# All mixers ahead of all feed-forward work, with gate and up as seven block products

## The chip, the cores and the metric

The kernel runs on one core of one Trainium2 chip. The metric is the device time of one execution in microseconds. Five engines work in parallel, each through its own instructions in a fixed order: PE (matrix products), DVE (VectorE), ACT (ScalarE), POOL (GpSimd), and SP, which here only starts DMA transfers. An engine that waits for another engine's result holds up everything behind it in its own order.

## The reference

One layer over 2048 prompt tokens and 32 sample tokens (8 sequences of 4), in float32:

```python
xn = _rmsnorm(h, norm_mix)
proj = xn @ w_in                                   # q, fg, iv, og (512 columns each), ca, cg
# group A: gated linear recurrence, 4 heads, state 128 x 128, chunks of 32 tokens
o, s_new = _hgrn2_scan(silu(q), 1 - forget, iv, log(forget), s0)
o_a = _rmsnorm(o, hgrn_out_norm) * silu(og)
# group B: u = ca * sigmoid(cg), depthwise convolution of width 31, LayerNorm over channels, silu
o_b = silu(layernorm(conv(u)))
h = h + concatenate([o_a, o_b]) @ w_out
xn2 = _rmsnorm(h, norm_ffn)
h = h + (silu(xn2 @ w_ffn_gate) * (xn2 @ w_ffn_up)) @ w_ffn_down      # 1024 -> 2816 -> 1024
gate = sigmoid(_rmsnorm(h, norm_ple) @ w_ple_gate)
h = h + gate * (p @ w_ple_proj)
y = _rmsnorm(h, norm_final)
```

Outputs are `y` and the end states of the recurrence and of the convolution, for prompt and samples.

## The kernel before

Features lie on partitions and tokens run along the columns of a tile. Every float32 operand of a product is split exactly into two parts that PE takes directly (`hi` and `lo`), and `mm3` (L511 to L513) makes each product of 128 rows by 128 columns from three matmuls, `hi*lo`, `hi*hi` and `lo*hi`. Weights come as pieces of 128 x 512: a DMA fills `raw`, ACT copies its high part to `wh` (L343), DVE subtracts for `wl` (L348). `wh`/`wl` lie in a ring of ten pairs.

The 2080 tokens are eight blocks, seven of 256 and a last one of 288 (with the samples). Two neighbouring blocks, the lanes, make a superblock. Per block there are four stages. First comes the in-projection `pm<-xa,w`. Then the mixer: the recurrence, whose small matmuls go to `px` banks, and the convolution, whose 31 taps per channel tile are DVE instructions `t<-u,cvw,t` and `h<-u,cvw,h` (L351). In blocks 0 and 1 every second tap's product is made by ACT into `ct` and only added by DVE. Then come the out-projection, which reads the same tiles `xa`, and the feed-forward: gate and up from `xb`, the activation in `xc`, the down-product, and at the end the embedding gate and projection. In the superblocks 1 and 2 both lanes share one product of 512 columns; superblock 0 takes mostly 256 columns at a time, superblock 3 takes 256 and 288. The residual `h` stays in SBUF (`hbuf`, four buffers) from the load of `x` to the store of `y`.

A list written out at build time (`seq`) gives the order of the weight pieces, and so of the big products; it places the in-products of superblock s+1 between the feed-forward products of superblock s. Each superblock loads and splits every weight again. A planner (`Sched`) runs all parts of the program as generators and puts each instruction into its engine's order by its expected start. Nothing is reordered at run time.

Of the kernel before, what the change touches and what calls it, by code (L numbers as in the profile page):

```python
# [7 lines left out]
F32 = mybir.dt.float32  # L8
# [5 lines left out]
D = 1024  # L14
# [18 lines left out]
CHUNKS = (4, 4, 4, 4, 2, 4)  # L33
AW = max(CHUNKS)
SOLO = 3
# [3 lines left out]
END = 0  # L39
SPLIT = 10  # L40
WS = 0
PSP = -1
TWO = (2, 1, 2, 2)
# [8 lines left out]
FILL = 1  # L52
ACTTAPS = 2
PCT = 500
AFTER = 12
LATE = 3
# [4 lines left out]
RANK = {"o": -2.0, "d": -1.0, "u": -0.5, "q": -0.5}  # L61
# [3 lines left out]
class Buf:  # L65
    """A tile (or a slice of one) and when its last writer and readers are expected to end."""
# [8 lines left out]
    def halves(self, n):  # L75
        """Two parts of n columns each, for two users; free() gives the whole back after both."""
# [16 lines left out]
class Sched:  # L93
    """Orders the instruction streams of concurrent generators by expected start, engine by engine.

    A generator yields op(...), acq(pool, n) or wait(event)."""
# [87 lines left out]
    def run(self):  # L184
        self.advance()
        while self.ready:
            best = {}
            for i, (th, req) in enumerate(self.ready):
                s = self.start(req)
                e = req[1]  # L190
                rank = (th[3] if th[0].__name__ == "lane" else -9.0) if e == "pe" else th[1]
# [21 lines left out]
        if self.blocked or any(p.waiting for p in self.pools):  # L213
# [22 lines left out]
def trunk(ctx: ExitStack, tc: tile.TileContext, x_in, p_in, s0_in, c0_in, w_in, w_out, w_gu, w_dn,  # L236
# [6 lines left out]

    def tl(name, shape, dt=F32):
        return sb.tile(shape, dt, name=name)

# [6 lines left out]
    idn = tl("idn", [128, 128])  # L253
    mask = tl("mask", [128, 128], I32)
    mask_s = tl("mask_s", [NS, NS], I32)
    bmask = tl("bmask", [NS, NB])
    gn_, lbt_, hgg_ = Buf(tl("gn", [128, 4, KD])), Buf(tl("lbt", [128, 2, HEADS])), Buf(tl("hgg", [128, 1]))
    cvw_, cvv_ = Buf(tl("cvw", [128, 4, CONV_W])), Buf(tl("cvv", [128, 3, 4]))
    gn, lbt, hgg, cvw, cvv = gn_.ap, lbt_.ap, hgg_.ap, cvw_.ap, cvv_.ap
    lbs = Buf(tl("lbs", [128, 4, HEADS]))  # L260
    lbx, lb, ha, hb = [lbs.ap[:, i, :] for i in range(4)]
    mhalf = tl("mhalf", [128, 4])
# [6 lines left out]
    zplace = [(2, 4 * b) if b < 2 else (resb[b], 0) for b in range(NBLK)]  # L269

    def pair(name, k):
# [118 lines left out]
    def toks(n):  # L390
        return [(t, min(128, n - t)) for t in range(0, n, 128)]

# [1 line left out]
    seq = []  # L394
    AB = (0, 1)
    J = (2,)
# [1039 lines left out]
```

## Time and profile before

| | |
|---|---|
| median of 3 runs | 2679.11 us (2678.74 to 2679.26) |
| profiled execution, span of its instructions | 2677.8 us |
| PE busy | 2644.3 us (99%), 15,904 recorded matmuls |
| DVE busy | 1885.8 us (70%) |
| ACT busy | 1184.2 us (44%) |
| DMA | 287.8 MB, mean 107 GB/s |

The median lies 1.3 us above the span of the profiled execution. Times of matmuls overlap in the records, since they are pipelined; the distance between starts tells what one costs in a row of many.

### The profile page before, as it was taken

To read this page: it belongs to the slowest core of one execution; us is meant where nothing else is said; L and a number is where in the kernel's file an instruction comes from. 1 tells how busy PE (TensorE), PEld (TensorE's weight loads), DVE (VectorE), ACT (ScalarE), POOL (GpSimd) and SP (SyncE) were. 2 spreads that over 40 slices of the span, in tenths; PEclk is the share of its full clock that TensorE was granted. 3 is DMA by queue.
4 is the path that set the end of the run, shared out by engine and by line. 5 is a ranking of instruction groups with operands and counts; after the bars stand their busy time and mean duration, and the time that the engine had idled before them with its cause. 6 is when DMAs were issued, how large, how long until landed. Compare 5 with 4: busy or idle time off the path is not lost.

```text
span 2677.8 us, 43961 instructions
## 1 busy us (share of the span) xinstructions
PE 2644.3 (99%) x15904; PEld 2310.5 (86%) x15904; DVE 1885.8 (70%) x4528; ACT 1184.2 (44%) x2717; POOL 130.2 (5%) x292
## 2 busy tenths in 40 slices
PE   7999999999999999999999999999999999999998
PEld 6999999877888878788888887788788799999997
DVE  8999876599988888457457887747667674333465
ACT  6776664435454543334344543333335433222242
POOL 0110000001000010000000000000000000000000
PEclk9999999999999999999999999999999999999999
DMA  3235555422234322222234423323232342222231
GB/s 128 80 128 176 187 186 181 124 87 74 85 127 153 98 74 96 86 92 88 91 94 133 130 85 97 109 85 96 89 99 95 120 136 87 80 87 86 89 103 58
DMA packets 169131, 287.82 MB, mean 107 GB/s; under 512 B 27088, under 2 KB 36816, under 8 KB 168912
## 3 DMA queue, kind: packets, MB, share of 16 engines
q1 hardware_dynamic: 168912, 285.01, 33.5%
q8 instruction: 124, 2.03, 0.3%
q14 instruction: 95, 0.78, 0.1%
HBM read 273.51 MB, written 11.43 MB: 106 GB/s over the span
## 4 chain that ended last, share of the span: by engine, by line
PE 95%; DVE 1%; issue 1%; DMA 1%; POOL 0%; ACT 0%; SPq 0%; POOLq 0%; DVEq 0%; ACTq 0%
PE pm L511 29%; PE pm L512 29%; PE pm L513 29%; PE pm L579 1%; PE pm L581 1%; PE pm L580 1%; PE px L1233 1%; PE px L1200 1%; PE px L1229 1%; PE px L1178 1%; DVE wl L348 0%; PE px L1265 0%; PE px L1256 0%; DMA h<-x_in 0%; PE px L1302 0%
## 5 line engine op out<-in xcount | busy, mean ns | idle before, releaser
L343 ACT ACTIVATE wh<-raw 128x512 fp32r<-128x512 f32 x968 | 605.3, 630 | 774.5 <-PE pm L512 597.9
L348 DVE TENSOR_TENSOR wl<-raw,wh 128x512 fp32r<-128x512 f32 x968 | 657.8, 688 | 353.0 <-ACT wh L343 345.2
L511 PE MATMUL pm<-xbl,wh 128*128 128x256 f32 (+2 forms) x2336 | 780.3, 334 | 1.5 <-ACT wh L343 1.2
L512 PE MATMUL pm<-xbh,wh 128*128 128x256 f32 (+2 forms) x2336 | 776.2, 332 | 0.0
L513 PE MATMUL pm<-xbh,wl 128*128 128x256 f32 (+2 forms) x2336 | 774.6, 332 | 0.4 <-DVE wl L348 0.4
L511 PEld LDWEIGHTS pm<-xbl,wh 128*128 128x128 f32 x2336 | 440.1, 188 | 54.0 <-issue 7.4
L513 PEld LDWEIGHTS pm<-xbh,wl 128*128 128x128 f32 x2336 | 438.9, 188 | 44.1 <-DVE wl L348 0.9
L512 PEld LDWEIGHTS pm<-xbh,wh 128*128 128x128 f32 x2336 | 439.5, 188 | 40.6
L511 PE MATMUL pm<-xal,wh 128*128 128x256 f32 (+2 forms) x1344 | 442.7, 329 | 2.6 <-DVE xal L348 2.6
L512 PE MATMUL pm<-xah,wh 128*128 128x256 f32 (+2 forms) x1344 | 433.4, 322 | 0.0
L513 PE MATMUL pm<-xah,wl 128*128 128x256 f32 (+2 forms) x1344 | 432.4, 322 | 0.0
L511 PE MATMUL pm<-xcl,wh 128*128 128x512 f32 (+2 forms) x1056 | 357.4, 338 | 3.0 <-DVE xcl L348 2.5
L512 PE MATMUL pm<-xch,wh 128*128 128x512 f32 (+2 forms) x1056 | 353.3, 335 | 0.0
L513 PE MATMUL pm<-xch,wl 128*128 128x512 f32 (+2 forms) x1056 | 353.3, 335 | 0.0
L511 PEld LDWEIGHTS pm<-xal,wh 128*128 128x128 f32 x1344 | 254.7, 190 | 28.5 <-DVE xal L348 3.5
L512 PEld LDWEIGHTS pm<-xah,wh 128*128 128x128 f32 x1344 | 254.4, 189 | 19.2
L348 DVE TENSOR_TENSOR h<-h,pm 128x256 f32<-128x256 f32 (+1 forms) x448 | 171.4, 422 | 141.2 <-PE pm L513 137.3
L513 PEld LDWEIGHTS pm<-xah,wl 128*128 128x128 f32 x1344 | 253.6, 189 | 19.4
L511 PEld LDWEIGHTS pm<-xcl,wh 128*128 128x128 f32 x1056 | 198.8, 188 | 25.5 <-DVE xcl L348 3.4
L513 PEld LDWEIGHTS pm<-xch,wl 128*128 128x128 f32 x1056 | 198.3, 188 | 20.5
L512 PEld LDWEIGHTS pm<-xch,wh 128*128 128x128 f32 x1056 | 198.8, 188 | 18.5
L351 DVE SCALAR_TENSOR_TENSOR t<-u,cvw,t 128x256 f32<-128x256 f32 x448 | 213.0, 476 | 0.0
(151 smaller groups left out, 2421.7 us busy)
## 6 DMA issues: line engine op xcount, KB each, us to landing
raw<-w_gu SPq DMA_DIRECT2D x416, 256.0 KB, 2.8
raw<-w_dn SPq DMA_DIRECT2D x200, 256.0 KB, 2.8
raw<-w_in SPq DMA_DIRECT2D x192, 256.0 KB, 2.8
raw<-w_out SPq DMA_DIRECT2D x80, 256.0 KB, 2.8
raw<-w_pg SPq DMA_DIRECT2D x64, 256.0 KB, 2.8
h<-x_in SPq DMA_DIRECT2D x14, 512.0 KB, 5.6
y<-h SPq DMA_DIRECT2D x28, 256.0 KB, 3.2
h<-x_in SPq DMA_DIRECT2D x20, 256.0 KB, 4.4
```

The costliest lines, as they stand in the source:

```text
L343: nc.scalar.activation(out, in_, func, scale=scale, bias=bias, **kw)
L348: return op("dve", d_tt(n), lambda: nc.vector.tensor_tensor(out=out, in0=a, in1=b, op=o), R, W)
L351: return op("dve", d_tt(n, not isinstance(s, float)), lambda: nc.vector.scalar_tensor_tensor(out=out, in0=a, scalar=s, in1=b, op0=o0, op1= ...
L511: nc.tensor.matmul(out, lhsT=wh, rhs=xl, start=first, stop=False)
L512: nc.tensor.matmul(out, lhsT=wh, rhs=xh, start=False, stop=False)
L513: nc.tensor.matmul(out, lhsT=wl, rhs=xh, start=False, stop=last)
L579: nc.tensor.matmul(bank.ap, lhsT=xs[0], rhs=wl, start=(k == 0), stop=False)
L580: nc.tensor.matmul(bank.ap, lhsT=xs[0], rhs=wh, start=False, stop=False)
L581: nc.tensor.matmul(bank.ap, lhsT=xs[1], rhs=wh, start=False, stop=(k == KD - 1))
L1178: nc.tensor.matmul(bs.ap[:, c], lhsT=kb.ap[:, c], rhs=q.ap[:, c], start=True, stop=True)
L1200: nc.tensor.matmul(bu[e].ap[:, c], lhsT=kt.ap[p, c], rhs=V[i].ap[p, hc], start=True, stop=True)
L1229: nc.tensor.matmul(bo.ap[:, c], lhsT=scst.ap[:, c], rhs=V[i].ap[:, hc], start=True, stop=False, skip_group_check=True)
```

## The change

The program now has two parts. In the first, all four superblocks go through in-projection, mixer and out-projection only. Superblock 0 loads and splits the weights as before and also writes both parts of each piece to DRAM (`wcache`); superblocks 1 to 3 read both parts from there and split nothing. The mixer's results have operand tiles of their own (`xo`), so in-products of s+1 can stand between the mixers and the out-products of s. All taps run on DVE. Each two feature tiles of the residual go to DRAM (`h1d`) after the out-products. Out-products of the last superblock are placed after the mixers' tiles have been freed (event `ffn`).

In the second part the 2080 tokens are three passes of 696, 696 and 688, each as two halves of 348 (or 344) columns. For gate and up of one 128-column tile of the hidden layer, the four blocks (gate and up, lower and upper half of the 1024 inputs, here `g0 g1 u0 u1`) times the four blocks of the operand (two halves of the inputs, two halves of the tokens) are made by seven block products instead of eight, in Winograd's form of Strassen's scheme. `combine` makes the seven operands per input tile from the normalised residual, `split2` makes the seven weight combinations, `gate_up` multiplies in the order `A12 A11 S1 S2 S4 S3 A22`, and `z_copies`, `z_low`, `z_high` make the sums. Down-product, embedding gate and projection are plain products for each half. Tiles of the second part reuse the first part's memory.

```diff
-CHUNKS = (4, 4, 4, 4, 2, 4)
+CHUNKS = (4, 4, 4, 4, 4, 2)
+HALF = (348, 348, 344)
+COMBOS = ("A12", "A11", "S1", "S2", "S4", "S3", "A22")
+NRING = 9
+NRAW = 6
-ACTTAPS = 2
...
     def split_weights():
+
         for i, (s, u, lanes) in enumerate(seq):
...
+                if not s:
+                    yield wait(("raw", i, a))
+                    raw = raw_of.pop((i, a))
+                    yield from split_piece(raw, hi, lo)
+                    S.release(raws, raw)
+                    S.spawn(keep_weights(kept, (hi, lo), ("kept", u, a)), 0)
+                else:
+                    yield wait(("kept", u, a))
+                    for c, t in zip(kept, (hi, lo)):
+                        yield dma(t.ap.bitcast(F32), c, W=[t], nbytes=512 * 512)
...
+            if s == NSUP - 1 and kind == "o":
+                yield wait("ffn")
...
+    def store_h1(b, m):
         n = blk_n(b)
...
+        idx = resb[b]
+        yield dma(h1d[:, m:m + 2, b * BLK:b * BLK + n], hbuf[idx][:, m:m + 2, 0:n], R=H[idx][m:m + 2],
+                  nbytes=1024 * n)
...
+    def gate_up(t, c, j, before):
+
+        z = (t, c, j)
+        bc = yield acq(main)
+        yield from strassen(*z, 0, "A12", bc, True)
+        if before:
+            yield from before
+        ba = yield acq(main)
+        yield from strassen(*z, 1, "A11", ba, True)
+        bb = yield acq(main)
+        S.spawn(z_copies(z, ba, bb), -3)
+        S.spawn(z_low(z, bc, bb), 0)
+        S.spawn(z_high(z, ba), 0)
+        yield from strassen(*z, 2, "S1", bb, True)
+        yield wait(("zc", z, "p1"))
+        yield from strassen(*z, 3, "S2", ba, False)
+        yield wait(("zc", z, "p5"))
+        yield from strassen(*z, 4, "S4", bb, False)
+        yield wait(("zc", z, "u2"))
+        yield from strassen(*z, 5, "S3", ba, False)
+
+        def rest():
+            yield wait(("zc", z, "c22"))
+            yield from strassen(*z, 6, "A22", ba, False)
+
+        return rest()
...
+    def z_copies(z, ba, bb):
+        n = HALF[z[0]]
+        for i, name, bank in ((1, "p1", ba), (2, "p5", bb), (3, "u2", ba)):
+            yield wait(("zp", *z, i))
+            q = yield acq(tmp2)
+            yield act(q.ap[:, 0:n], bank.ap[:, 0:n], AF.Copy, R=[bank], W=[q], n=n)
+            zt[z, name] = q
+            S.fire(("zc", z, name))
...
+    def z_high(z, ba):
+        n = HALF[z[0]]
+        yield wait(("zp", *z, 5))
+        yield wait(("zc", z, "p5"))
+        p5 = zt.pop((z, "p5"))
+        p5a = p5.ap[:, 0:n]
+        yield tt(p5a, ba.ap[:, 0:n], p5a, ALU.add, R=[ba, p5], W=[p5], n=n)
+        S.fire(("zc", z, "c22"))
...
+        yield from put(a12, "A12")
+        yield from put(a11, "A11")
+        yield sum_(s, a21, a22, ALU.add)
+        yield from put(s, "S1")
+        yield from put(a22, "A22")
+        S.release(tmp2, a22)
+        yield sum_(a21, a11, a21, ALU.subtract)
+        yield sum_(a11, s, a11, ALU.subtract)
+        yield from put(a11, "S2")
+        yield sum_(s, a12, a11, ALU.subtract)
+        S.release(tmp2, a12, a11)
+        yield from put(s, "S4")
+        S.release(tmp2, s)
+        yield from put(a21, "S3")
+        S.release(tmp2, a21)
...
+    S.fire("ffn")
+    S.spawn(load2(), 1)
+    S.spawn(split2(), SPLIT)
```

How instructions move shows at three places. The first is PE's order around the LayerNorm of the last block. `px<-idn,h` with 128x128 or 32x128 are transposes of the convolution's result `h` to tokens and, in the second group, back; `xb` is gate and up's operand. Before:

```order
L1041 MATMUL px_173<-idn,h_74 128x128 x4
L1041 MATMUL px_176<-idn,h_74 128x128 x4
L1041 MATMUL px_174<-idn,h_74 32x128 x4
L511 MATMUL pm_172<-xbl,wh_94 128x512
L512 MATMUL pm_172<-xbh,wh_94 128x512
L513 MATMUL pm_172<-xbh,wl_95 128x512
...
L1073 MATMUL px_175<-idn,h_74 128x128 x2
L1073 MATMUL px_175<-idn,u_124 128x32
```

After, with `xa` the last in-products' operand and `xo` that of the out-products:

```order
L527 MATMUL pm_174<-xah,wl_95 128x288
L1136 MATMUL px_177<-t_151,t_149 32x128 x2
L1145 MATMUL px_176<-t_148,t_153 128x256
...
L921 MATMUL px_176<-idn,h_78 128x128 x4
L921 MATMUL px_177<-idn,h_78 128x128 x4
L921 MATMUL px_175<-idn,h_78 32x128 x4
L1182 MATMUL px_176<-idn,t_146 128x128 x2
...
L953 MATMUL px_175<-idn,u_144 128x32
L525 MATMUL pm_171<-xol,wh_96 128x256
```

Before, 51 big matmuls of 512 columns stand between the two groups of transposes. After, nothing but small matmuls of the mixers (55 rows) stands between the last in-product and the first out-product.

The second place is DVE at the step into the feed-forward of a superblock. Before, the rows are from superblock 0: `h` is scaled by the norm (L351) and `xbl`, the low part of gate and up's operand, follows:

```order
L348 TENSOR_TENSOR wl_89<-raw_103,wh_88 128x512
L351 SCALAR_TENSOR_TENSOR h_75<-h_75,gn,px_173 128x256 x2
L351 SCALAR_TENSOR_TENSOR t_128<-h_72,gn,px_175 128x256
L351 SCALAR_TENSOR_TENSOR t_129<-h_72,gn,px_175 128x256
L351 SCALAR_TENSOR_TENSOR t_133<-h_72,gn,px_175 128x256
L351 SCALAR_TENSOR_TENSOR t_127<-h_72,gn,px_175 128x256
L348 TENSOR_TENSOR xbl<-t_128,xbh 128x256
```

After, from the last residual addition of the out-products (`h_78`, 288 columns) into pass 0; `f` and `h_77` hold squares of `norm2`, and the two reductions are the sums of the first half's tokens:

```order
L373 TENSOR_TENSOR h_78<-h_78,px_177 128x288
L373 TENSOR_TENSOR tw_105<-raw_102,tw_105 128x512
L373 TENSOR_TENSOR wl_89<-tw_105,wh_88 128x512
L373 TENSOR_TENSOR f_9008<-f_9008,h_77 128x348
L373 TENSOR_TENSOR wl_87<-raw_100,wh_86 128x512
L373 TENSOR_TENSOR f_9007<-f_9007,f_9008 128x348
L1613 MEMSET sm_68 128x1
L373 TENSOR_TENSOR wl_91<-raw_101,wh_90 128x512
L1622 TENSOR_REDUCE sm_68<-px_178 128x2
L1625 TENSOR_REDUCE sm_68<-px_178 92x1
L376 SCALAR_TENSOR_TENSOR h_77<-h_77,f_9009 128x348
```

The whole norm of pass 0 and all of `combine` follow the last out-products in this order, and no big product of another stage is left for PE in between.

The third place is PE in one gate and up tile of pass 0, with bank and buffer numbers; the rows shown are the first matmul of each block product, and each stands for twelve (four input tiles by three):

```order
L1354 MATMUL px0_175<-xal_107,wh4_88 128x348
...
L1354 MATMUL pm0_171<-xal_107,wh5_90 128x348
...
L1354 MATMUL px0_175<-xal_107,wh6_92 128x348
...
L1354 MATMUL pm0_171<-xal_107,wh7_94 128x348
...
L1354 MATMUL pm1_172<-xal_107,wh0_80 128x348
...
L1354 MATMUL pm0_171<-xal_107,wh8_96 128x348
```

Two banks now alternate block by block within a tile, and between two block products into the same bank its content is copied by ACT or added by DVE; before, a bank took its 24 matmuls in a row and was then evacuated. The fifth row is the next tile's first product, placed ahead of this tile's last.

## Rows read from the trace of the kernel before

**Rows 1.** The page: busy time of each engine, and PE's granted clock in 40 slices.

```profile
PE 2644.3 (99%) x15904; PEld 2310.5 (86%) x15904; DVE 1885.8 (70%) x4528; ACT 1184.2 (44%) x2717; POOL 130.2 (5%) x292
...
PEclk9999999999999999999999999999999999999999
```

**Rows 2.** The page: chain that ended last, by engine and by line.

```profile
PE 95%; DVE 1%; issue 1%; DMA 1%; POOL 0%; ACT 0%; SPq 0%; POOLq 0%; DVEq 0%; ACTq 0%
PE pm L511 29%; PE pm L512 29%; PE pm L513 29%; PE pm L579 1%; PE pm L581 1%; PE pm L580 1%; PE px L1233 1%; PE px L1200 1%; PE px L1229 1%; PE px L1178 1%; DVE wl L348 0%; PE px L1265 0%; PE px L1256 0%; DMA h<-x_in 0%; PE px L1302 0%
```

**Rows 3.** Windows: stretch, length, busy time of each engine, clock, DMA share, GB/s.

```profile
0.00:67.00 67.00, 53.34 (x326) 46.86 (x327) 58.59 (x169) 46.66 (x108) 6.64 (x22) 1.00 0.40 127
67.00:134.00 67.00, 67.00 (x568) 63.65 (x567) 63.17 (x174) 49.90 (x135) 11.24 (x28) 1.00 0.25 80
134.00:200.00 66.00, 66.00 (x562) 64.06 (x561) 60.79 (x153) 49.46 (x126) 7.52 (x18) 1.00 0.39 127
...
2200.00:2400.00 200.00, 200.00 (x1597) 199.78 (x1596) 86.10 (x173) 60.52 (x120) 1.23 (x1) 1.00 0.28 90
```

**Rows 4.** Timeline of PE at the start: start, duration, line and tiles.

```profile
14.84 0.58 PE L511 MATMUL pm<-xal,wh 128*128 128x256 f32 x1 [2.43 <-DVE xal L348]
...
17.40 0.41 PE L512 MATMUL pm<-xah,wh 128*128 128x256 f32 x1
...
18.89 0.41 PE L513 MATMUL pm<-xah,wl 128*128 128x256 f32 x1
```

**Rows 5.** Timeline of the end.

```profile
2665.06 0.29 PE L513 MATMUL pm<-xch,wl 128*128 128x288 f32 x1
...
2670.72 3.49 DVE L351 SCALAR_TENSOR_TENSOR h<-h,gn,px 128x288 f32<-128x288 f32 x8 [1.95 <-PE px L839]
2671.68 2.88 SPq L462 DMA_DIRECT2D y<-h  x4
```

**Rows 6.** Timeline of PE in two stretches of big products.

```profile
1149.66 0.39 PE L511 MATMUL pm<-xbl,wh 128*128 128x512 f32 x1
...
1155.93 0.39 PE L511 MATMUL pm<-xbl,wh 128*128 128x512 f32 x1
...
2249.96 0.30 PE L511 MATMUL pm<-xbl,wh 128*128 128x288 f32 x1
...
2251.96 0.28 PE L511 MATMUL pm<-xcl,wh 128*128 128x256 f32 x1
...
2254.79 0.30 PE L511 MATMUL pm<-xbl,wh 128*128 128x288 f32 x1
```

**Rows 7.** Groups by line and shape, PE: the feed-forward's products, one line of three.

```profile
L511 PE MATMUL pm<-xbl,wh 128*128 128x512 f32 x992 | 396.2, 399 | 0.0
...
L511 PE MATMUL pm<-xbl,wh 128*128 128x256 f32 x928 | 261.2, 281 | 1.5 <-ACT wh L343 1.2 <-DVE h L348 0.2
...
L511 PE MATMUL pm<-xcl,wh 128*128 128x512 f32 x480 | 191.7, 399 | 0.0
...
L511 PE MATMUL pm<-xbl,wh 128*128 128x288 f32 x416 | 122.9, 295 | 0.0
...
L511 PE MATMUL pm<-xcl,wh 128*128 128x256 f32 x384 | 109.0, 284 | 3.0 <-DVE xcl L348 2.5 <-DVE h L348 0.3
...
L511 PE MATMUL pm<-xcl,wh 128*128 128x288 f32 x192 | 56.7, 295 | 0.0
```

**Rows 8.** Groups by line and shape, DVE: weight low parts and taps.

```profile
L348 DVE TENSOR_TENSOR wl<-raw,wh 128x512 fp32r<-128x512 f32 x968 | 657.8, 688 | 353.0 <-ACT wh L343 345.2
L351 DVE SCALAR_TENSOR_TENSOR t<-u,cvw,t 128x256 f32<-128x256 f32 x448 | 213.0, 476 | 0.0
...
L351 DVE SCALAR_TENSOR_TENSOR h<-t,cvw,h 128x32 f32<-128x32 f32 x60 | 14.6, 244 | 0.0
```

**Rows 9.** Timeline of DVE: two taps one behind the other.

```profile
90.95 0.88 DVE L351 SCALAR_TENSOR_TENSOR t<-u,cvw,t 128x256 f32<-128x256 f32 x2
```

**Rows 10.** Costliest groups, ACT: weight high parts.

```profile
L343 ACT ACTIVATE wh<-raw 128x512 fp32r<-128x512 f32 x968 | 605.3, 630 | 774.5 <-PE pm L512 597.9
```

More of the change, by code (lines that the diff above doesn't have):

```diff
@@ L182, in start, with run @@
         return t
-    def run(self):
+    def run(self, last=True):
         self.advance()
@@ L487, in load_weights @@
             src = unit_src(u)
-            for a in range(pieces(u)):
+            for a in range(2 if not s else 0):
                 raw = yield acq(raws)
@@ L916, in stage_x @@
     def stage_x(b):
-        for x in range(b - 1):
-            yield wait(("lnread", x))
+        yield wait(("n1", 1, HOLD))
         for k in range(0, KD, 4):
@@ L1341, in trunk, with cut, flat @@
     S.spawn(lane(1), 30)
-    with tc.manual_schedule():
-        S.run()
+    manual = tc.manual_schedule()
+    manual.__enter__()
+    S.run(False)
+    assert len(tmp.free) == 8 and len(hg.free) == 10 and len(misc.free) == 4
+    scope["guard"].__exit__(None, None, None)
+    open_scope("ffn")
+    def cut(tiles, count):
+        return [tuple(Buf(t[:, i * WID:(i + 1) * WID]) for t in tiles) for i in range(count)]
+    def flat(i, count):
+        f = hbuf[i].rearrange("p k t -> p (k t)")
+        return [Buf(f[:, j * WID:(j + 1) * WID]) for j in range(count)]
@@ new lines, in mm3s, with strassen @@
+    def mm3s(out, wh, wl, xh, xl, first, last):
+        for i, (a, b) in enumerate(((wh, xl), (wh, xh), (wl, xh))):
+            nc.tensor.matmul(out, lhsT=a, rhs=b, start=first and i == 0, stop=last and i == 2, skip_group_check=True)
+    def strassen(t, c, j, i, name, bank, first):
+        n = HALF[t]
+        key = ("z", t, c, j, i)
+        yield wait(("w2", key))
+        w = w2.pop(key)
+        for kp in range(KP):
+            yield wait(("x2", t, kp, name))
+            x = X2[kp][name]
+            col = slice(kp * 128, (kp + 1) * 128)
+            args = (bank.ap[:, 0:n], w[0].ap[:, col], w[1].ap[:, col], x[0].ap[:, 0:n], x[1].ap[:, 0:n],
+                    first and kp == 0, kp == KP - 1)
+            yield op("pe", 3 * d_mm(n), lambda a=args: mm3s(*a), R=[*w, *x], W=[bank])
+        S.release(ring, w)
+        S.fire(("zp", t, c, j, i))
@@ new lines, in row, with norm2, get @@
+    def row(n, get, r, ev):
+        bank = yield from rms2(n, get)
+        yield act(r.ap[:, 0:n], bank.ap[:, 0:n], AF.Copy, R=[bank], W=[r], n=n)
+        S.release(misc, bank)
+        S.fire(ev)
+    def norm2(t):
+        if t:
+            yield wait(("a", t - 1, 2, 0, 1))
+        for h in HALVES:
+            def get(k, h=h):
+                q = yield acq(tmp2)
+                yield from h1_load(t, h, k, q)
+                return q, q
+            yield from row(HALF[t], get, r2[h], ("r2", t, h))
+        if t:
+            yield wait(("a", t - 1, last_chunk, CHUNKS[-1] - 1, 1))
+        for kp in range(KP):
+            five = yield acq(tmp2, 5)
+            S.spawn(combine(t, kp, five), 0)
```

730 lines of the change are left out of this document (481 added, 249 removed).

## The prediction, made before the changed kernel ran

> **What bounds the kernel now.** I read the busy times first: PE is busy for 2644.3 of 2677.8 us, at full clock in every slice [rows 1]. The chain that ended last says the same from the other side: 95% of it is PE, and 87% are the three lines of `mm3` [rows 2]. Then I read windows, because DVE's 70% is an average over unlike stretches: in the first 200 us, where convolution and weight splitting meet, DVE is busy for 182.6 us (58.59 + 63.17 + 60.79), 91%, and late in the feed-forward for 86 of 200 [rows 3]. So the time is the number of matmuls times their pace, plus a start of 14.8 us [rows 4] and an end of 12.6 us, from the end of the last product (2665.06 + 0.13) to 2677.8 [rows 5]. The change must show itself as fewer columns through PE, and as new stretches in which PE has nothing to do.
>
> **What it removes and adds on PE.** The pace is taken start to start. With 512 columns, 27 intervals lie between 1149.66 and 1155.93: 0.2322 us. With 288, 15 between 2249.96 and 2251.96: 0.1333. With 256, 24 between 2251.96 and 2254.79: 0.1179 [rows 6]. The three lie close to a line, which gives 0.160 us at 348 columns and 0.158 at 344, widths that no row shows. If a column cost what it costs at 512, a pass would be cheaper by 1.1%; as at 288, dearer by 1%.
>
> Feed-forward products before, each row three times for the three lines [rows 7]: (992 + 480) x 3 = 4416 of 512 columns, 1025 us; (928 + 384) x 3 = 3936 of 256, 464 us; (416 + 192) x 3 = 1824 of 288, 243 us. Sum 1732.6. After, one pass has 22 tiles x 7 block products x 4 input tiles x 3 = 1848 for gate and up (eight blocks would be 2112), 22 x 8 x 2 x 3 = 1056 for down, 8 x 8 x 2 x 3 = 384 for the embedding gate and 96 for its projection: 3384. Two passes at 0.1598 and one at 0.1580 make 1616.2 us (1598 to 1632 by the two bounds). That is **116 us less**. Of it 126 us come from the eighth block (792 matmuls x 0.16); the change of widths gives back 10.
>
> The rest of PE's stretch, 2665.2 - 14.8 - 1732.6 = 917.8 us, is the mixers' products, the small matmuls and whatever small waits there are. The mixers' products keep their number and widths, so I keep it. Start, this rest and the new feed-forward make 2548.8 us. Now the stretches without cover.
>
> **Mixers alone.** DVE loses most weight splits there: only 64 pieces are split, three quarters of the mixers' pieces come back from DRAM. It gains the taps that ACT made. In the changed order 2207 DVE instructions stand ahead of the last out-products. A tap takes 476 ns [rows 8], but two in a row end after 0.88 us [rows 9], so each costs 0.40 start to start; the same 0.07 is taken off the others. 928 taps make 371 us, 116 sample taps at 0.17 make 20, 64 low parts at 0.61 make 39. The other 1099 lie between 0.17 (narrow) and 0.42 (256 columns); I take 0.29, 319 us. Sum about 750 us, or 820 at the 91% density of [rows 3], against some 855 us at which PE ends its last in-product (14.8 + 917.8, less 48 for the last out-products, 192 of 256 and 192 of 288 columns, and some 30 for small matmuls of the feed-forward). PE stays ahead, narrowly. Only in superblock 0, which also splits, is DVE late: its work up to the last tap of block 1 comes to some 252 us, which is 288 us after the start at that density, LayerNorm included, where PE has run through what it was given at about 281; with the transposes and splits behind it I take **18 us** (0 to 45). In-products of s+1 stand right behind those of s and read the same `xa`, so at three places PE waits for the first splits: **5 us** (0 to 20).
>
> Superblock 0 reads 256 KB and writes 512 KB for each piece, 49 MB in some 280 us, 175 GB/s; the trace moved 127 GB/s at a share of 0.40 [rows 3], so the queues would be near 0.55 busy, and I put nothing on it.
>
> **The last mixer.** Before, 51 products of 512 columns cover the LayerNorm of the last block (the first order above), nearly 12 us. After, PE has only small matmuls there. DVE has 146 instructions left after the last in-product: 31 wide taps (12.4 us), 60 narrow (10), 55 others at 0.28 (15), 38 us together; transposes back, activation and split add 6. About 10 of these 44 us are small matmuls already counted in the rest: **34 us** (15 to 55).
>
> **Into the feed-forward.** After the last addition of the out-products, DVE's order (second place above) has the end of the norm of pass 0, first for one half, then the other: reductions, power on POOL, broadcast. At the end of the program that chain takes 5.5 us from the last product to the first scaled tile [rows 5]; two of them with copies between make 14. Then `combine` stands: some 39 DVE instructions ahead of the fourth `A12`, at 0.45, 18 us. **32 us** (20 to 50): the products have nothing else to do. Later passes have the previous pass's embedding and down-products as cover, so they cost nothing unless the operands' tiles come free late. A cold clock comes with both idle stretches: products of 256 columns at the start take (18.89 - 17.40)/7 = 0.213 us, nearly double [rows 4], until about 6 us after the first; half of such a stretch is lost each time, **6 us** for two.
>
> **Within the feed-forward.** Per tile DVE has seven low parts and four differences of weights (11 x 0.61) and seven operations of 348 columns (0.44): 9.8 us, against 84 x 0.16 = 13.4 on PE. ACT has seven high parts of 630 ns [rows 10] and seven operations of 348 columns, some 7 us. Neither is the bound. A copy between two block products of one bank has the twelve matmuls of the other bank as cover, 1.92 us; it takes about 0.45, behind at most one other instruction of 0.69. I take **8 us** for all 66 tiles and the pass ends (0 to 70).
>
> **The end.** 5.5 us of chain, 16 scalings of 348 columns at 0.5 (before: 8 in 3.49 us [rows 5]) and a store of 3: **17 us**.
>
> Sum: 2548.8 + 18 + 5 + 34 + 32 + 6 + 8 + 17 = 2668.8 us of span. The median lies 1.3 us above the profiled span, so **2670 us**.
>
> At 512 columns the trace has a product each 0.232 us [rows 6]. A rule of the Trainium skill would have it faster: "TensorE: Matmul & The Clock Gate", section "Back-to-back issue gap", gives a lone stream of matmuls of N columns N/2.4 ns plus 2.5 at full clock, 216 ns at 512. The trace disagrees. By that rule 348 columns would take 147.5 ns and the feed-forward's products about 1492 us, an estimate from that page.
>
> **The rivals.**
>
> *The waits are mostly hidden (20%).* The estimates of 34 and 32 us assume DVE works through its order without gaining on PE. If the out-products already cover most of the norm, and DVE is done with the taps when the last in-product ends, 15 and 15 remain, and superblock 0 costs nothing. 2548.8 + 5 + 15 + 15 + 4 + 5 + 16 = 2609; with half of that saving 2640. I name 2625.
>
> *The mixers become DVE-bound (13%).* 750 us of DVE work, less the 38 behind, must end with PE's last in-product at about 855 + 18 + 5. That holds down to a density of 0.83. At 0.78, with more waits between engines than in [rows 3] because no feed-forward fills the gaps, it ends 45 us later: 2715.
>
> *Each gate and up tile waits (13%); slower than before.* Each tile has four waits for ACT or DVE under a cover of 1.92 us, in engines that are over half full and in fixed order. If the releasing instruction stands behind two weight operations of 0.6 us, the wait is not covered. At 0.22 us each, 264 waits make 58 us, less the 8: 2720. From 0.065 us each on (17 us in all) the kernel is no faster than before.
>
> *The pace gets better (2%).* At full clock, 2.4 GHz, 512 columns at one a cycle take 0.213 us and 348 take 0.145; [rows 6] stand 0.019 above that at 512, 0.013 at 288 and 0.011 at 256. If most of this excess hangs on the order of banks and weights and goes with the new one, the products save up to 0.015 x 10,152 = 150 us: 2520. Nothing in the rows speaks for it; the excess is there in both stretches. The page's rule above is a milder form of this case.
>
> **How the numbers follow.** 52% remain for my sum, with a range of its own of 2650 to 2692. A change below 0.2%, 5.4 us, can hardly be told from none: same is 2673.8 to 2684.5. Of my own case about half lies below, three tenths within, a fifth above. Faster: 0.27 + 0.20 + 0.02 and a small part of the DVE case, 0.51. Same: 0.16 + 0.02, 0.18. Slower: 0.31. The range reaches from the hidden case's lower half to the slower rivals: **2612 to 2720**.
>
> **What would show it.** Products of 348 columns at 0.160 us start to start; 10,152 of them. PE idle of 20 us or more at three places: out-products of superblock 0, behind the last in-product (ended by `xo`), ahead of the first block product (ended by `xa`). Between block products no idle over 0.1 us in most tiles. DVE at 85% to 92% through the mixers. I am wrong if `z_copies` or the `c22` addition ends many waits of PE, if PE's idle in the mixers is spread over in-products and named DVE, or if the three places together stay under 40 us.

## The result and the profile after

The changed kernel takes 2725.1 us (median of four runs, 2720.45 to 2728.98), the kernel before on the same chip 2679.2. The ratio is 1.0171, with an interval of 1.0157 to 1.0186: **slower by 46 us**, where 2670 had been forecast. The profiled execution has a span of 2723.3 us and a mean granted clock of 0.968.

The page: engine, busy time, share of the span, instructions; then the granted clock in 40 slices, and the chain that ended last.

```profile
PE 2566.1 (94%) x15886; PEld 2409.8 (88%) x15886; DVE 1999.1 (73%) x4506; ACT 1071.4 (39%) x2397; POOL 134.1 (5%) x286
...
PEclk9999899999998679999999899999999999999998
...
PE 89%; DVE 6%; DMA 2%; POOL 1%; ACT 1%; issue 1%; SPq 0%; DVEq 0%; POOLq 0%; ACTq 0%
```

PE lost 78 us of busy time against [rows 1], and still the span grew by 45.5: PE now stands still for 157.2 us where it stood still for 33.5. The clock row shows where (a slice is 68.1 us): dips in slice 5 (272 to 340 us), in slices 13 to 15 (817 to 1021) and in slice 23 (1498 to 1566), the end of the first pass. The windows were laid around these and around the end (stretch, its length, busy time and count of PE, PEld, DVE, ACT and POOL, granted clock, DMA share, GB/s):

```profile
0.00:281.00 281.00, 263.67 (x1799) 232.74 (x1800) 255.91 (x696) 134.62 (x364) 34.12 (x92) 0.99 0.66 228
281.00:300.00 19.00, 9.64 (x63) 7.40 (x61) 18.93 (x51) 5.59 (x17) 3.18 (x6) 0.74 0.21 69
300.00:600.00 300.00, 298.56 (x1559) 242.81 (x1560) 246.91 (x682) 93.66 (x283) 38.07 (x78) 0.99 0.60 199
600.00:860.00 260.00, 256.13 (x1649) 219.60 (x1648) 199.13 (x592) 72.25 (x215) 29.18 (x69) 1.00 0.52 166
700.00:800.00 100.00, 99.34 (x595) 81.60 (x594) 64.05 (x203) 16.27 (x50) 6.15 (x21) 1.00 0.59 187
860.00:935.00 75.00, 44.61 (x182) 28.09 (x182) 56.04 (x190) 15.64 (x53) 8.12 (x23) 0.59 0.27 76
985.00:1036.00 51.00, 17.47 (x69) 14.37 (x69) 37.56 (x84) 21.60 (x48) 1.71 (x2) 0.60 0.42 130
1482.00:1512.00 30.00, 19.50 (x102) 18.22 (x101) 30.00 (x65) 20.02 (x44) 0.00 (x0) 0.77 0.21 63
2698.00:2723.30 25.30, 3.52 (x17) 2.05 (x15) 13.02 (x31) 1.33 (x3) 1.70 (x2) 0.61 0.36 112
```

Up to 860 us PE is short of work once only, around 281. Then come 75 us with PE busy for 45, and 51 us with 17. The eye should stop at 700 to 800: PE is full, but DVE, which has the convolution to do, is busy for 64 of 100 us, and 70 us later PE has run out of work. What PE's waits are called (engine, line, what it waited for: us in total, times, longest):

```profile
PE px L1136 <- DMA t<-s_in: 22.8, 8, 4.4
PE pm L1354 <- DVE xal L373: 14.9, 3, 8.6
PE px L1618 <- DVE sm L1613: 14.2, 3, 7.6
PE pm L527 <- DVE wl L373: 14.1, 2, 8.7
PE pm L525 <- ACT wh L368: 10.3, 1, 10.3
...
PE px L1354 <- DVE h L373: 5.5, 9, 0.6
...
PE pm L1354 <- DVE h L373: 1.8, 3, 0.6
...
PE pm L1354 <- DVE f L373: 1.2, 2, 0.6
```

L1136 multiplies by the recurrence's states of the samples, which are loaded for the purpose (`s_in`). L1354 is the block product, L1618 the transposes in a norm's sum over features. The last three rows are the wait for `c22`: fourteen times, 8.5 us in all, in 66 tiles. They stand only at tiles with a down-product behind them, where no product of a next tile is placed ahead of the last block product; there are fifteen of these.

The mile-posts, from PE's timeline (start, duration, engine, line, operation):

```profile
867.51 0.29 PE L527 MATMUL pm<-xah,wl 128*128 128x288 f32 x1
...
871.34 0.42 PE L1136 MATMUL px<-t,t 128*32 128x128 f32 x1 [3.54 <-DMA t<-s_in]
...
934.05 0.58 PE L525 MATMUL pm<-xol,wh 128*128 128x256 f32 x1
...
1200.03 0.33 PE L525 MATMUL px<-xol,wh 128*128 128x348 f32 x1
...
1203.70 0.32 PE L527 MATMUL pm<-xoh,wl 128*128 128x348 f32 x1
...
2698.44 0.32 PE L527 MATMUL pm<-wh,wl 128*128 128x344 f32 x1
```

The last in-product starts at 867.51 and the first out-product 66.5 us later. Between 1200.03 and 1203.70 lie 23 intervals of 0.1596 us. The last product starts at 2698.44, and 24.7 us follow from its end to the span's. The last out-product starts at 984.44; the first block product starts at 1006.9, and the hundredth at 1042.9, where a hundred in a row would need 15.8.

What happens in this gap, from the timelines of SP, ACT and DVE (`h`, `f` hold loaded residual tiles and squares; `r` is the norm):

```profile
990.14 0.91 SPq L454 DMA_DIRECT2D h<-h1d  x2
...
991.87 0.46 ACT L368 ACTIVATE r<-px 128x348 f32<-128x348 f32 x1 [3.90 <-PE px L1633]
994.39 0.98 ACT L368 ACTIVATE h<-h 128x348 f32<-128x348 f32 x2 [2.06 <-DMA h<-h1d]
995.38 1.50 ACT L368 ACTIVATE f<-f 128x348 f32<-128x348 f32 x3
...
995.91 0.52 DVE L376 SCALAR_TENSOR_TENSOR h<-h,f 128x348 f32<-128x348 f32 x1 [5.91 <-ACT f L368]
...
1003.36 2.06 DVE L376 SCALAR_TENSOR_TENSOR f<-f,gn,r 128x348 f32<-128x348 f32 x4 [2.36 <-ACT r L368]
...
1006.32 0.94 DVE L373 TENSOR_TENSOR xal<-f,xah 128x348 fp32r<-128x348 f32 x2
```

The first half's norm is done at 992.3. SP issues the second half's eight loads only from 990.1 on, and its squares, sums and reductions follow the first half's norm: each load waits for a free buffer in `get`, and the two halves follow each other in one generator.

The end of the first pass, DVE:

```profile
1482.84 1.07 DVE L376 SCALAR_TENSOR_TENSOR hxl<-h,gn,hxh 128x348 fp32r<-128x348 f32 x2
1483.82 0.51 DVE L373 TENSOR_TENSOR xal<-h,xah 128x348 fp32r<-128x348 f32 x1
1484.25 0.51 DVE L373 TENSOR_TENSOR f<-h,f 128x348 f32<-128x348 f32 x1
1484.68 0.51 DVE L373 TENSOR_TENSOR h<-pm,h 128x348 f32<-128x348 f32 x1
...
1505.56 0.68 DVE L373 TENSOR_TENSOR wl<-raw,wh 128x512 fp32r<-128x512 f32 x1
```

DVE is busy for all 30 us of this window. The next pass's operands (`xal`, `f<-h,f`) stand among the last residual additions and the operand of the embedding gate (`hxl`), all ahead of the embedding's first `wl` at 1505.56; PE gets its weights 10.3 us late. At the third pass's end, where no next pass follows, 5.4 us of such a wait remain (2619.57).

The very end, SP's queue of stores, the row that answers to the last of [rows 5]:

```profile
2705.47 15.53 SPq L454 DMA_DIRECT2D y<-h  x32
```

Where four stores were issued after the last norm, 32 now are, 0.485 us each; DVE is through with its 16 scalings (7.82 us) before half of the stores are out.

### The profile page after: what moved, and what is told of

It reads as the page before. It is cut to its first block, busy times and chain, and to the rows that moved or that the text cites. A ratio compares the mean times of both kernels' runs of the same rounds, so it can differ in the third digit from the quotient of the medians.

```text
span 2723.3 us, 43381 instructions
## 1 busy us (share of the span) xinstructions
PE 2566.1 (94%) x15886; PEld 2409.8 (88%) x15886; DVE 1999.1 (73%) x4506; ACT 1071.4 (39%) x2397; POOL 134.1 (5%) x286
## 4 chain that ended last, share of the span: by engine, by line
PE 89%; DVE 6%; DMA 2%; POOL 1%; ACT 1%; issue 1%; SPq 0%; DVEq 0%; POOLq 0%; ACTq 0%
PE pm L1354 20%; PE pm L525 14%; PE pm L527 13%; PE pm L526 13%; PE px L1354 12%; PE px L525 3%; PE px L527 3%; PE px L526 3%; DVE h L373 1%; PE pm L593 1%; PE pm L595 1%; PE pm L594 1%; DVE h L376 1%; DMA t<-s_in 1%; PE px L1113 1%; PE px L1080 1%
## 5 line engine op out<-in xcount | busy, mean ns | idle before, releaser
L373 DVE TENSOR_TENSOR wl<-raw,wh 128x512 fp32r<-128x512 f32 x520 | 356.4, 689 | 200.0 <-ACT wh L368 197.1
L368 ACT ACTIVATE wh<-raw 128x512 fp32r<-128x512 f32 x520 | 323.2, 627 | 380.7 <-PE pm L526 208.2
L527 PE MATMUL pm<-xoh,wl 128*128 128x348 f32 (+4 forms) x1072 | 350.0, 326 | 14.1 <-DVE wl L373 14.1
L525 PE MATMUL pm<-xol,wh 128*128 128x348 f32 (+4 forms) x1072 | 353.7, 330 | 1.9 <-DVE xol L373 1.6
L526 PE MATMUL pm<-xoh,wh 128*128 128x348 f32 (+4 forms) x1072 | 349.6, 326 | 0.0
L1354 PE MATMUL pm<-xal,wh 128*128 128x348 f32 (+1 forms) x661 | 213.6, 323 | 18.0 <-DVE xal L373 14.9
L527 PEld LDWEIGHTS pm<-xoh,wl 128*128 128x128 f32 x1072 | 205.5, 192 | 20.3 <-DVE wl L373 14.7
L368 ACT ACTIVATE wh<-tw 128x512 fp32r<-128x512 f32 x198 | 124.8, 630 | 244.2 <-DVE tw L373 120.5
L525 PEld LDWEIGHTS pm<-xol,wh 128*128 128x128 f32 x1072 | 205.7, 192 | 12.1 <-issue 3.8
L1354 PE MATMUL pm<-xah,wh 128*128 128x348 f32 (+1 forms) x661 | 212.6, 322 | 0.0
L1354 PE MATMUL pm<-xah,wl 128*128 128x348 f32 (+1 forms) x661 | 212.4, 321 | 0.0
L526 PEld LDWEIGHTS pm<-xah,wh 128*128 128x128 f32 x960 | 182.1, 190 | 12.1
```

Source lines behind the costliest of these rows:

```text
L368: nc.scalar.activation(out, in_, func, scale=scale, bias=bias, **kw)
L373: return op("dve", d_tt(n), lambda: nc.vector.tensor_tensor(out=out, in0=a, in1=b, op=o), R, W)
L525: nc.tensor.matmul(out, lhsT=wh, rhs=xl, start=first, stop=False)
L526: nc.tensor.matmul(out, lhsT=wh, rhs=xh, start=False, stop=False)
L527: nc.tensor.matmul(out, lhsT=wl, rhs=xh, start=False, stop=last)
L1354: nc.tensor.matmul(out, lhsT=a, rhs=b, start=first and i == 0, stop=last and i == 2, skip_group_check=True)
```

## The experiments

Theory: PE's saving is real, and it is lost in stretches where no product covers the chain of the other engines; what sets such a stretch is the order in which DVE, ACT and the loads come, not how much DVE has to do. Rival: DVE has too much to do in all (1999 us busy), and order only moves the loss. Differences between kernels are taken from the ratios, times 2679 us; the kernel before took 2678.8 to 2680.1 in the three sets. A ratio's interval reaches some 4 us to either side, so a difference of 5 us is not clear of the noise.

**The samples' states a step ahead.** The load of the next state is issued before the work on this one:

```diff
-            for g in range(4):
+            def state(g):
                 s0 = yield acq(tmp)
...
+                return s0, s3
+            ahead = yield from state(0)
+            for g in range(4):
+                s0, s3 = ahead
+                if g < 3:
+                    ahead = yield from state(g + 1)
```

> Edit: the samples' old states are loaded one step ahead, so that each load has a tile of its own and stands ahead of the store of the step before. In the changed kernel PE waits 22.8 us in 8 waits for these loads. Theory 1 (the lost time is PE's stretches without cover, and they add up): the stretch behind the last in-product shrinks from 66 us to 42 to 48 us, the kernel comes to 2698 to 2710. Rival (the stretch is bound by DVE's taps, which fill it as well): it shrinks by less than 6 us, 2717 to 2725.

Measured: 1.0154 (1.0138 to 1.0171), 2721.5 us. PE's waits from 860 to 940 of this kernel:

```profile
PE px L921 <- DVE h L373: 9.6, 2, 6.2
PE px L953 <- DVE h L384: 4.3, 2, 2.3
PE px L1143 <- DMA t<-s_in: 4.2, 3, 2.5
```

The wait for the states fell from 22.8 us to 4.2, and the kernel gained 4.6, which is not clear of the noise. The stretch from the last in-product to the first out-product (868.4 to 932.8) is 64 us long, where it was 66.5. That is what the rival expected: the convolution's result (`h`, L921 transposes it) now comes last. Its window says why:

```profile
890.00:920.00 30.00, 14.45 (x45) 7.29 (x44) 25.81 (x98) 3.72 (x13) 2.77 (x4) 0.50 0.18 46
```

DVE is busy for 25.8 of 30 us. Two chains of nearly one length end here, and the largest row of the waits named only the later one.

**Loads of pass 0 on ACT's queue, both halves side by side.**

```diff
-                yield from h1_load(t, h, k, q)
+                yield from h1_load(t, h, k, q, dma if t else dma_a)
...
-            yield from row(HALF[t], get, r2[h], ("r2", t, h))
+            if t:
+                yield from row(HALF[t], get, r2[h], ("r2", t, h))
+            else:
+                S.spawn(row(HALF[t], get, r2[h], ("r2", t, h)), 0)
```

> Edit: the loads of the first pass's norm and operands are issued by ACT instead of SP, both halves at once, so that norm and operand sums stand among the last out-products in DVE's order. Theory 1: the idle between the last out-product and the first block products (50 us until all four input tiles are there) falls to 10 to 20 us, 2685 to 2700. Rival (DVE or the loads are the limit in this stretch anyway): under 10 us saved, 2714 to 2725.

Measured: 1.0154 (1.0139 to 1.0169), 2720.7 us: 4.6 us, again within the noise, a miss. The first block product does come earlier, at 997.3 and 0.6 us behind the last out-product, but the out-products took 61.4 us (50.4 in the changed kernel), with 5.5 us of waits for their weights from DRAM. ACT's timeline shows that the edit put load and use on one engine, each use ahead of the next load:

```profile
951.99 0.49 ACT L371 ACTIVATE h<-h 128x348 f32<-128x348 f32 x1 [2.23 <-DMA h<-h1d]
952.00 0.35 ACTq L460 DMA_DIRECT2D h<-h1d  x1
954.30 0.49 ACT L371 ACTIVATE h<-h 128x348 f32<-128x348 f32 x1 [1.82 <-DMA h<-h1d]
954.31 0.38 ACTq L460 DMA_DIRECT2D h<-h1d  x1
```

**Chunks of the hidden layer in the order of before.**

```diff
-CHUNKS = (4, 4, 4, 4, 4, 2)
+CHUNKS = (4, 4, 4, 4, 2, 4)
```

> Edit: the last two down-product chunks change places (4 then 2 tiles becomes 2 then 4), so the last down-product of a pass has 192 matmuls (30.7 us) in place of 96 (15.4 us) over the same 16 residual additions and 16 operand splits on DVE (16 us). Theory 1: the three waits at the ends of the passes (10.3, 8.7 and 5.4 us) go, with the cold clock behind them 25 to 40 us, 2685 to 2700. Rival (the waits there come from the norm's chain or from weights): no more than 8 us, 2715 to 2725.

Measured: 1.0173 (1.0158 to 1.0188), 2725.4 us: nothing gained. The 5.4 us of the third pass's end are gone; around the first pass's end waits of 7.0, 4.5 and 3.0 us (`wl`, a norm's power, `h`) stand in place of the 10.3.

**Eight plain products in place of seven.** The order of the two parts stays; gate and up are made by `mm3` with the 16 operands of before:

```diff
-        yield from strassen(*z, 0, "A12", bc, True)
...
+        for up_ in range(2):
+            for h in HALVES:
+                bank = yield acq(main)
+                for i in range(2):
+                    for kp in range(KP):
...
+                        yield op("pe", 3 * d_mm(n), lambda a=args: mm3(*a), R=[*w, *x], W=[bank])
+                S.spawn((u_plain if up_ else g_plain)(z, h, bank), 0)
```

> Edit: gate and up as eight plain block products (1.14 times their matmuls: 792 more, 126 us) in the same two-part program, no combinations of weights and operands. Theory 1 (the seven products save what their count says, the loss lies elsewhere): 2823 to 2850, a little under +126 since DVE has less to do at the start and the ends of the passes. Rival (waits between block products of one bank eat the saving): +60 or less, 2725 to 2785.

Measured: 1.0520 (1.0504 to 1.0536), 2818.6 us, 93 us more than with seven. The 792 matmuls are worth 126 at 0.16; some 33 come back. At the start of the feed-forward 8 do (from the last out-product the hundredth product lies 34.9 us further than its own time, not 42.6). PE's waits at the ends of the passes are 11 us less, and the 9 us in the tiles are gone; the other 5 are not traced. So the seven products cost a quarter of what they save, and the new order of the stages, with plain products, is 139 us slower than before, of which the change of widths is 10.

**Out-products of superblock 2 later.** Eight more in-product units of the last superblock come first, so that its convolution gets its inputs earlier:

```diff
-        add(s + 1, todo[:AFTER], then)
+        after = 20 if s == NSUP - 2 else AFTER
+        add(s + 1, todo[:after], then)
```

> Edit: the out-products of superblock 2 stand behind 20 of the last superblock's 24 in-product units instead of behind 12. In the changed kernel DVE is idle for a third of 700 to 800 us, while these out-products run and no convolution has its input, and the taps of the last two channel tiles start only at 858.6 and 890.2. Theory 2 (the end of the mixers is late because DVE gets its last inputs late, not because it has too much work): the first out-product of the last superblock starts 15 to 25 us earlier, 2700 to 2710. Rival (DVE's sum of work decides): under 5 us, 2719 to 2725.

Measured: 1.0126 (1.0111 to 1.0141), 2713.0 us, 12 us less than the changed kernel and a little short of the expectation. The window of 700 to 800:

```profile
700.00:800.00 100.00, 97.28 (x642) 83.28 (x642) 75.08 (x232) 20.95 (x66) 9.64 (x28) 0.97 0.52 157
```

DVE is busy for 75 us, not 64, and the first out-product of the last superblock starts at 922.2, 12 us earlier. So 11 of DVE's 36 us of idle time there were want of inputs. After the last in-product's start DVE has 27.6 us of work left, where it had 49.1.

**Loads ahead and both halves at once at the start of the feed-forward.** A loader of its own runs ahead on SP's queue, and `combine` issues its four loads before its first scaling:

```diff
+    def ahead0():
+        for k in range(KD):
+            for h in HALVES:
+                q = yield acq(tmp2)
+                yield from h1_load(0, h, k, q)
...
+        if t == 0:
+            S.spawn(ahead0(), -5)
...
             yield from h1_load(t, h, k, q)
+        for q, k, h in ((a21, kp, 1), (a22, kp + KP, 1), (a11, kp, 0), (a12, kp + KP, 0)):
             qa = q.ap[:, 0:n]
```

> Edit: in the first pass the 16 loads of the norm go out ahead of their use, both halves side by side, and the four loads of an input tile's operands stand ahead of its first scaling; in the run with ACT's queue the squares still came one load at a time, some 2 us each. Theory 2 (the start of the feed-forward is a chain of load, square, load): the first block product starts at most 8 us after the last out-product and idle before steady products is 15 us or less in place of 50, 2690 to 2705. Rival (DVE's work for norm, operands and weights is the limit, about 45 us of it): 2712 to 2722.

Measured: 1.0109 (1.0094 to 1.0124), 2708.9 us, 16.6 us less and 4 above the expected range. The first block product starts at 985.98, directly behind the last out-product at 985.85. What waits remain there:

```profile
PE pm L1354 <- DVE xal L373: 9.5, 1, 9.5
PE pm L1354 <- DVE x2l L373: 6.4, 1, 6.4
```

The norm is hidden; `combine`, one operand after the other, is not.

**The next pass's operands after the embedding's first result.**

```diff
             yield wait(("a", t - 1, last_chunk, CHUNKS[-1] - 1, 1))
+            yield wait(("h3", t - 1, 0, 1))
```

> Edit: the operands of the next pass are made only after the first embedding output, not between the last down-product and the embedding. In the changed kernel DVE is busy without a gap from 1482 to 1512 with the sums and splits of the next pass standing among the residual additions, and the embedding's first weights wait behind them. Theory 2 (order on DVE at the pass end, not the amount): the waits of 10.3 and 8.7 us at the first two pass ends fall under 4 us each, 2700 to 2712. Rival (the same DVE work only moves to the start of the next pass and PE waits there): 2719 to 2727.

Measured: 1.0203 (1.0188 to 1.0219), 2734.1 us: 9 us more. From 1440 to 1570 PE waits 5.3 us for `wl` and 7.2 us, in three waits, for ACT's `f` (L368), the activation of an embedding gate, which frees a bank and now stands behind the splits of the next pass's operands. The sum is the 12 us of before under other names. The rival had expected this at the start of the next pass; it came within the embedding.

**The four together** (states ahead, out-products later, loads ahead, operands later):

> All of the last three edits and the prefetch of sample states together. Theory 2: the savings add, 2640 to 2670, faster than the kernel before. Rival (the stretches hide one another): 2690 or more.

Measured: 1.0057 (1.0040 to 1.0074), 2696.7 us, 30.5 us less than the changed kernel, a miss: the time lies in the rival's range. Its reason does not hold, though. Singly the four sum to 4.6 + 12.1 + 16.6 - 8.6 = 24.7, so they do not hide one another; they were worth less than expected.

**Convolution inputs first.** In the last superblock all products that feed the convolution's first channel tile (`ca0 cg0`) come first and the others between those of the recurrence; with later out-products, states and loads ahead, without the later operands:

```diff
+        if s == NSUP - 2:
+            todo = []
+            for w in "ca0 cg0 iv f0 q0 ca1 cg1 f1 q1 ca2 cg2 f2 q2 ca3 cg3 f3 q3 og0 og1 og2 og3".split():
+                todo += [(w[:2].rstrip('0123'), int(w[-1]))] if w[-1] in '0123' else [(w, j) for j in range(4)]
```

> Edits: prefetched sample states and the early loads of the first pass (as in the runs before), and in the last superblock the in-products start with the first convolution tile's two units, with the out-products of superblock 2 after 20 units; the operands of the next pass are left where the changed kernel has them. Theory 2 (the three edits that order DVE's work earlier add, the fourth gave 9 us back): 2683 to 2692. Rival (the stretches hide one another, as the late operands' pass ends did not): 2697 or more.

Measured: 0.9997 (0.9988 to 1.0006), 2679.0 us, 4 below the expected range: **order alone gives back all 46 us**, with DVE busy for 1996.3 us, hardly less than before. The last in-product starts at 881.3, the first out-product at 904.5: 23 us, where 66.5 lay, and DVE has 16.2 us of work in them. The hundredth block product starts at 992.5, 50 us earlier, so the whole gain lies ahead of it. The window of 860 to 935, at a granted clock of 0.84 where it was 0.59:

```profile
860.00:935.00 75.00, 63.95 (x425) 55.63 (x424) 43.50 (x133) 18.55 (x49) 4.06 (x10) 0.84 0.65 204
```

**The same with the chunks of before.** Only `CHUNKS = (4, 4, 4, 4, 2, 4)` is added:

> The kernel of e9 with the last two down-product chunks exchanged (2 then 4 tiles). In e3 that took away the wait at the end of the third pass (5.4 us) and moved those of the other two. With the operand loads out of the way the same DVE work stands behind 192 matmuls. Theory 2: 5 to 12 us under e9. Rival (DVE's amount at a pass end is the limit): within 3 us of e9.

Measured: **0.9946 (0.9933 to 0.9960), 2666.5 us, faster than both kernels**. Its page, the row of busy times:

```profile
PE 2550.8 (96%) x15886; PEld 2401.2 (90%) x15886; DVE 1998.7 (75%) x4506; ACT 1073.6 (40%) x2397; POOL 133.2 (5%) x286
```

Its window from 700 to 800:

```profile
700.00:800.00 100.00, 99.40 (x681) 84.49 (x680) 85.10 (x259) 25.51 (x78) 11.79 (x36) 1.00 0.53 160
```

PE's timeline at its step into the feed-forward:

```profile
961.53 0.29 PE L532 MATMUL pm<-xoh,wl 128*128 128x288 f32 x1
961.66 0.32 PE L1366 MATMUL pm<-xal,wh 128*128 128x348 f32 x1
```

DVE's busy total is that of the changed kernel (1998.7 against 1999.1), and the time is 60 us less. From 700 to 800 DVE is busy for 85 us. The edit that gave nothing by itself gives 14 here. In the trace the hundredth block product starts at 997.75, 5 us later than without it, though the edit concerns only the down-products: the planner places everything anew. The gain comes behind, where PE's waits from 1000 us on sum to 34.0 us instead of 41.5. Why the same edit did nothing in the changed kernel no run shows.

**Sums of operands on POOL.** The kernel with convolution inputs first, with `sum_` moved from DVE (16 sums a pass):

```diff
-            return tt(out.ap[:, 0:n], a.ap[:, 0:n], b.ap[:, 0:n], o, R=[a, b], W=[out], n=n)
+            return op("pool", 700.0, lambda: nc.gpsimd.tensor_tensor(
+                out=out.ap[:, 0:n], in0=a.ap[:, 0:n], in1=b.ap[:, 0:n], op=o), [a, b], [out])
```

> The kernel of e9 with the four operand sums of each input tile (16 a pass, 128x348) on POOL instead of DVE. It takes 7 us of work from DVE at each pass start, where DVE is busy without a gap. If DVE's amount is the limit there: 8 to 15 us under e9. If POOL's longer instruction or its latency stands in the chain: the same or up to 20 us over e9.

Measured: 1.0035 (1.0022 to 1.0047), 2689.6 us, 10 us more than with the sums on DVE. The sums lie in the chain, and POOL's part of it is longer (POOL's busy time rose by 55 us for 48 sums, about 1.1 us each, against 0.51 on DVE). DVE was not relieved either: it has 48 instructions fewer and is busy for 2005.5 us, where it was busy for 1996.3. Beside a sum on POOL its own instructions take longer:

```profile
982.46 1.25 POOL L1708 TENSOR_TENSOR f<-h,f 128x348 f32<-128x348 f32 x1 [0.52 <-DVE x2l L373]
982.84 1.25 DVE L373 TENSOR_TENSOR x2l<-f,x2h 128x348 fp32r<-128x348 f32 x1
...
984.61 0.51 DVE L373 TENSOR_TENSOR x2l<-f,x2h 128x348 fp32r<-128x348 f32 x1
```

So this run does not test what less work for DVE is worth.

**No low parts of the feed-forward's weights.** The changed kernel, with some 650 of DVE's instructions left out:

```diff
-                        yield from split_piece(src, *e)
+                        yield act(e[0].ap, src.ap, AF.Copy, R=[src], W=[e[0]], n=512)
...
-            args = (bank.ap[:, 0:n], w[0].ap[:, col], w[1].ap[:, col], x[0].ap[:, 0:n], x[1].ap[:, 0:n],
+            args = (bank.ap[:, 0:n], w[0].ap[:, col], w[0].ap[:, col], x[0].ap[:, 0:n], x[1].ap[:, 0:n],
```

> The changed kernel with the feed-forward's low weight parts left out: no DVE subtraction for them, and the matmuls that read a low part read the high part, so PE's work is the same and the values are not. It takes 652 instructions of 0.61 us, some 400 us, from DVE, nothing from PE. If DVE's amount of work makes PE's waits at the start of the feed-forward and at the pass ends: 2690 to 2705 (the waits of 10.3, 8.7 and 5.4 us gone, 5 to 10 us at the start). If the order and the chains make them: 2715 or more.

Measured: 1.0117 (1.0103 to 1.0130), 2711.7 us: about 400 us of DVE's work gone, 14 us gained. At the first pass's end PE is now nearly full:

```profile
1482.00:1512.00 30.00, 28.08 (x172) 26.96 (x171) 29.65 (x67) 22.58 (x50) 0.00 (x0) 1.00 0.30 92
```

The time lies between the two expected ranges. The run does not separate amount from place at the passes' ends: `wl`, for which PE waited there, is itself among what is left out. Ahead of the first block products the waits stayed nearly as they were (`xal` 15.0 us, 14.9 in the changed kernel); the norms' `sm` went from 14.2 to 12.5.

## Why the prediction was wrong

| | forecast, us | measured, us |
|---|---|---|
| up to the last in-product's start | 867.6 | 867.5 |
| from there to the first out-product | 44 | 66.5 |
| out-products | 51 | 50.4 |
| to the hundredth block product, beyond its products | 35 | 42.6 |
| the rest of the feed-forward | 1654 | 1671 |
| end | 17 | 24.7 |

The first row is the sum 14.8 + 917.8 - 48 - 30 - 10 + 18 + 5. That it agrees to 0.1 us is luck: the 30, 18 and 5 are rough estimates. Half of the forecast for clock is added to rows 3 and 4 each.

**What held.** The pace is 0.1596 us at 348 columns, where 0.160 was read off three other widths. The rule of the Trainium skill quoted beside the sum ("TensorE: Matmul & The Clock Gate", section "Back-to-back issue gap") would give 0.1475; the trace disagrees as it did at 512. The Trainium skill states that rule for matmuls by themselves; for a stream that loads weights before each, as here, the same section has about 131 ns at 512 columns, and the trace of the kernel before has 232. Of the two bounds of the pace, 1598 and 1632 us, the rows give 1596 and 1629, which changes nothing. Superblock 0 cost some 14 us, from 286.2 to 300.5 without a big product (18). Block tiles hardly wait, so the rival on the slower side, 264 waits in the tiles, did not come: fourteen waits, 8.5 us. The waits were not mostly hidden, and the pace did not get better.

**What failed first: "the last mixer", 34 us and 10 of small matmuls; 66.5 were measured.** The step took DVE to be through with all but 38 us of its work when the last in-product ended, since its sum of 750 us fits into 855 at 91% density. The sum was nearly right: DVE was busy for 720.9 us up to 860 and 56 more to 935, 777 in all. But density is an effect of order. It fell to 77% from 600 to 860 and to 64% from 700 to 800, because out-products of superblock 2 held PE's queue while the convolution had no inputs. So the stretch of 66.5 us holds 49.1 us of DVE's work instead of 38, and 17.5 in which DVE stands still instead of 6. Of these, 9.1 are waits for products of the recurrence (L1145), which stand behind a second chain that the step did not have at all, eight loads of states, each waited for; alone its removal was worth 4.6 us, within the noise, since the first chain ended as late. Feeding the convolution earlier gave 12 us by itself, and with the whole order the stretch fell to 23 us, with 16.2 of DVE's work in it.

The rival of mixers bound by DVE named this place, with more waits in general as its reason, where the runs show one place. Its price was 45 us, twice the 22.5 that this stretch was too long; that its 2715 came near 2725 is luck, since the rest was lost elsewhere.

**"Into the feed-forward", 32 us and 3 of cold clock: 42.6.** The norm took 18.9 us (984.45 to 1003.36), with DVE busy for 8.8 of them, where 14 were forecast: the loads were left out, and the second half began when the first was done. `combine` then had 47 DVE instructions ahead of the fourth `A12`, 21.6 us, where 39 and 18 were forecast. Ordering the loads ahead and the halves side by side took 16.6 us off; this step was mis-sized through its order too.

**"Within the feed-forward", 8 us: 8 + 17.** The waits in the tiles, 8.5 us, are as forecast. The missing part is the ends of the passes, waits of 10.3, 8.7 and 5.4 us, with lower clock behind them. The small matmuls of this stretch (L1618 and L1633) were busy for 14 us, where 30 were put down, so the waits, 33 us with the tiles, are more than the difference of 17 shows. "Later passes have the previous pass's embedding and down-products as cover" holds for PE, but the same operands stood in DVE's order ahead of the embedding's weights and so took the cover away; at the third end there are no such operands, and residual additions and splits alone make the 5.4. The step asked what covers the new work, not what the new work delays.

**"The end", 17 us: 24.7.** The store of 3 us was the price of the last one before; now 32 are issued at 0.485 us each, and they last longer than the scalings. This is read from the trace; no run changed it.

The four terms are 22.5 + 7.6 + 17 + 7.7 = 55 us too low; they make the difference of spans, 2723.3 against 2668.8.

**Still open.** States ahead, later out-products and loads ahead gain 33 us singly, and with convolution inputs first 46.6. How much of the remaining 13 is that order, and how much the three together, no run separates. Whether amount counts beside order at the ends of passes the runs don't show. In the fastest version PE still waits 16 us for `xal` and `x2l` ahead of the first block products.

## What to carry to other kernels

A saving on the engine that bounds a kernel is paid out only where the other engines' work stays covered; each place where the change takes the cover away has to be priced by walking the other engines' orders row by row, the loads and every store's issue included, and not from their sums and mean density. Where an engine is about to be waited for, look for the time before at which it stood idle: order gave back 46 us here with DVE's work unchanged, and taking 400 us of its work away gave 14. An edit that gains nothing alone may gain beside others (chunks: 0 us, then 14), so keep it for a second try.

## What the runs showed of the hardware

That uncovered stretches are paid for twice was expected at two places and came at more. The granted clock, after PE had stood idle for much of the stretch, was 0.59 from 860 to 935, 0.60 from 985 to 1036 and also 0.77 around the first pass's end, means between the levels of 1.2 and 2.4 GHz, and 1.00 from 700 to 800, where PE was full. With the stretch after the last in-product shortened to 23 us, the same window of 860 to 935 was granted 0.84. And a store costs its issue: 0.485 us on SP on average for each of the last 32, which carry 28 to 144 KB. In the run with the sums on POOL a DVE instruction on 128x348 that ran beside such a sum took 1.25 us instead of 0.51.
